# Gate products on quarters of the array and a half-array second score pass in a hybrid RG-LRU and attention step

## The chip, the cores and the metric

The kernel runs on one core of a Trainium2 chip. The metric is device time in microseconds (us) of one execution; the lower the better. Five engines of the core work side by side and wait for one another through semaphores: TensorE (PE in the profile, with its weight loads listed apart as PEld), VectorE (DVE), ScalarE (ACT), GpSimd (POOL) and SyncE (SP), which issues most of the DMAs. TensorE is an array of 128 rows by 128 columns. A product loads a stationary operand into the array (a weight load) and streams a moving operand through it; the contraction runs over the rows, that is over the partitions of both operands, and each column of the array gives one partition of the output, in an accumulation memory called PSUM. PSUM has eight banks of 128 partitions by 512 float32 values here.

## The reference

One inference step of one layer over 2048 prompt tokens and 8 decode tokens, model width 1024. What matters for this change:

```python
z = einsum('btd,de->bte', rmsnorm(x), w_in)
xr, gr, q, k, v = split(z)             # 512, 512, 512, 128, 128 columns
# recurrence group: 8 blocks of 64 channels
xc = causal_conv(xr)
r = sigmoid(block_diag(xc, gate_a_w) + gate_a_b)   # each block its own 64x64 matrix
i = sigmoid(block_diag(xc, gate_x_w) + gate_x_b)
a = exp(-8 * r * softplus(-lru_lambda))
h = scan(h * a + sqrt(1 - a**2) * (i * xc))
rec = h * gelu(gr)
# attention group: 8 heads of 64, 2 key/value heads, window 128, learned sinks
s = einsum(q, k) / 8                   # per head, 128 queries against 256 keys
att = softmax(concat(mask(s), sink)) @ v
h = x + concat(rmsnorm(rec), rmsnorm(att)) @ w_out
y = h + (silu(rmsnorm(h) @ w_gate) * (rmsnorm(h) @ w_up)) @ w_down
```

A final normalisation gives the outputs, beside the new key/value windows and recurrence states.

## The kernel before

Activations are held with channels on partitions and tokens along the free axis. The tokens are worked through in four groups `s` (520 tokens in the first, as two column blocks of 260; 512 in each of the other three). For each group there are 14 units of the input projection (`unit`, matmuls at L281 to L283), a recurrence chain for each of four chunks `c` of 128 channels (`rec_chunk`), attention in items of 128 queries and one key/value head (`attn_item`, 32 items), and the output projection. The feed-forward part follows, from about 620 us on, in three groups of two column halves; the change does not touch it.

Large products are made from rounded pieces: an operand x is split into a rounded part (hi) and the rest (lo), both in a float32 format that TensorE takes in one instruction, and hi·hi, hi·lo and lo·hi are added in PSUM. Products in plain float32 take two instructions each.

*The gates.* The 64x64 matrices of two neighbouring blocks stand on the diagonal of a 128x128 matrix in `gw`, whose other quarters are zero. For each chunk, gate and column block, L608 makes one full-array float32 product `ps = gw.T @ xc` in the single bank of the pool `ps_m` (`m_tile`), and L610 turns it into `ra` or `ia` with a tanh on ScalarE. The same bank serves several other small products.

*The scores.* For an item, `qst` holds four heads' queries with the hi part on the 64 partitions `hr` of its key/value head and the lo part on the other 64 (`lr`). `KK` holds the keys' hi part on both halves of the partitions, so one 128-row product (L767) gives hi·hi + lo·hi. `KL` holds the keys' lo part on `hr` and zeros on the other half, so the second 128-row product (L768) adds hi·lo. The scores of two heads share a bank of the pool `ps_s` (two banks, `s_tile`): heads 0 and 1 in the first, 2 and 3 in the second. L771 on VectorE scales and masks them out of PSUM.

*What sets the order.* All pieces of work are Python generators, each with planned times (`T_IP`, `D_REC`, `D_ATT` and others) that become priorities; `with ahead()` raises a product's priority by a fixed lead. A list scheduler then simulates the program and puts out on each engine the ready instruction of the best priority. What is written in sequence can so be separated in an engine's queue if an operand or a bank of one part is ready later. Each engine works through its queue in the order that comes out.

Of the kernel before, what the change touches and what calls it, by code (L numbers as in the profile page):

```python
# [12 lines left out]
P = 128  # L13
# [177 lines left out]
def hybrid_step(tc, xT, xR, vecs, cst, gatew, win, wout, wgate, wup, wdown, kT, vC, ck, cv, sconv, sh0,  # L191
# [4 lines left out]
    with ExitStack() as ctx:  # L196
# [26 lines left out]
        def o_tile(name):  # L223
            return ps_o.tile([P, 512], F32, tag="o", name=name)

        def m_tile(name):
            return ps_m.tile([P, 512], F32, tag="m", name=name)

# [211 lines left out]
        with ExitStack() as actx:  # L440
# [3 lines left out]
            ap2 = A(tc.tile_pool(name="ap2", bufs=2))  # L444
            ap3 = A(tc.tile_pool(name="ap3", bufs=2))

            gw = ap1.tile([P, 1024], F32, name="gw")
            hist = ap1.tile([P, CR, 3], F32, name="hist")
            nc.vector.memset(hist, 0.0)
            carry = ap1.tile([P, CR], F32, name="carry")  # L450
# [2 lines left out]
            sh = ap1.tile([P, CR, NB], F32, name="sh")  # L453
            KK = ap1.tile([P, 2, 640], F32R, name="KK")
            KL = ap1.tile([P, 2, 640], F32R, name="KL")
            nc.gpsimd.memset(KL[64:128, 0, :].bitcast(F32), 0.0)
            nc.gpsimd.memset(KL[0:64, 1, :].bitcast(F32), 0.0)
            qraw = ap1.tile([P, G, TM], F32, name="qraw")
            rrec = ap1.tile([P, CR, TM], F32, name="rrec")
            ratt = ap1.tile([P, CR, TM], F32, name="ratt")  # L460
# [116 lines left out]
            def rec_chunk(s, c):  # L577
                _, T, nbl, _, _ = SUBS[s]
                prev = (("h", s - 1, c),) if s else ("prologue",)
                yield (ip_time(s, c) - 9,) + ((("xr", s - 1, c),) if s else ())  # L580
                xr = ap3.tile([P, TM + 3], F32, tag="xr", name=f"xr{s}_{c}")
                nc.gpsimd.tensor_copy(xr[:, 0:3], hist[:, c, :])
                yield from unit(s, c, xr[:, 3:])
                t = ip_time(s, c) + U_IP
                yield t
                nc.gpsimd.tensor_copy(hist[:, c, :], xr[:, 512:515])
                fire(("xr", s, c))
                cw = [col(V_CW + c * 4 + j) for j in range(4)]
                xc = rt("xc", f"xc{s}_{c}")
                nc.scalar.activation(xc[:, :512], xr[:, 0:512], AF.Identity, bias=col(V_CB + c), scale=cw[0])  # L590
                if T > 512:
                    nc.scalar.activation(xc[:, 512:T], scv[:, c, 0, :], AF.Identity, bias=col(V_CB + c), scale=cw[0])
                for j in (1, 2, 3):
                    n = T if j == 3 else 512
                    nc.vector.scalar_tensor_tensor(xc[:, :n], xr[:, j:j + n], cw[j], xc[:, :n], ALU.mult, ALU.add)
                    if T > 512 and j < 3:
                        nc.vector.scalar_tensor_tensor(xc[:, 512:T], scv[:, c, j, :], cw[j], xc[:, 512:T],
                                                       ALU.mult, ALU.add)
                if T > 512:
                    nc.scalar.dma_start(sconv_o[:, c, 2, :], xr[:, 515:515 + NB])  # L600
                yield (t + D_REC[0], "prologue")
                ra = rt("ra", f"ra{s}_{c}")
                ia = rt("ia", f"ia{s}_{c}")
                for gi, (dst, hb) in enumerate(((ra, hab), (ia, hxb))):
                    for n0, nn in nbl:
                        ps = m_tile(f"g{s}_{c}_{gi}_{n0}")
                        with ahead():
                            nc.tensor.matmul(ps[:, :nn], gw[:, (gi * 4 + c) * P:(gi * 4 + c + 1) * P], xc[:, n0:n0 + nn],  # L608
                                             start=True, stop=True)
                        nc.scalar.activation(dst[:, n0:n0 + nn], ps[:, :nn], AF.Tanh, bias=hb[:, c:c + 1], scale=0.5)  # L610
                yield t + D_REC[1]
                ix = ap2.tile([P, TM], F32, tag="ix", name=f"ix{s}_{c}")
                nc.vector.scalar_tensor_tensor(ix[:, :T], ia[:, :T], 1.0, xc[:, :T], ALU.add, ALU.mult)
                pair = (s, c >> 1)
                second = pair in q2s
                a = ia if second else ap1.tile([P, TM], F32, tag="a", name=f"a{s}_{c}")
                if not second:
                    q2s[pair] = q2_tile(f"q2{s}_{c >> 1}")
                q2 = q2s[pair][:, c & 1, :]
                nc.scalar.activation(a[:, :T], ra[:, :T], AF.Exp, bias=nc2[:, c:c + 1], scale=nc2[:, c:c + 1])  # L620
                nc.scalar.activation(ra[:, :T], ra[:, :T], AF.Tanh, bias=c2[:, c:c + 1], scale=c2[:, c:c + 1])
                nc.scalar.square(q2[:, :T], a[:, :T])
                nc.vector.scalar_tensor_tensor(q2[:, :T], q2[:, :T], 1.0, ra[:, :T], ALU.add, ALU.mult)
                if second:
                    yield pair_time(s, c) + T_REC
                    both = q2s[pair][:, :, :T]
                    nc.scalar.activation(both, both, AF.Sqrt)
                    fire(("sqrt",) + pair)
                yield (pair_time(s, c) + T_REC + 2 * (c & 1), ("sqrt",) + pair, ("gr", s, c)) + prev
                nc.vector.scalar_tensor_tensor(ix[:, :T], q2[:, :T], 0.5, ix[:, :T], ALU.mult, ALU.mult)  # L630
                h = q2
                nc.vector.tensor_tensor_scan(h[:, :512], a[:, :512], ix[:, :512],
                                             carry[:, c:c + 1], ALU.mult, ALU.add)
                nc.gpsimd.tensor_copy(carry[:, c:c + 1], h[:, 511:512])
                if T > 512:
                    nc.vector.tensor_tensor(h[:, 512:T], a[:, 512:T], sh[:, c, :], ALU.mult)
                    nc.vector.tensor_tensor(h[:, 512:T], h[:, 512:T], ix[:, 512:T], ALU.add)
                    nc.scalar.dma_start(sh_o[:, c, :], h[:, 512:T])
                gr = rrec[:, c, :]
                nc.vector.scalar_tensor_tensor(gr[:, :T], gr[:, :T], 0.5, h[:, :T], ALU.mult, ALU.mult)  # L640
                fire(("h", s, c))
# [51 lines left out]
            def k_chunk(s):  # L693
# [10 lines left out]
                nc.vector.tensor_copy(KK[0:64, 1, m], kr[64:128, :512])  # L704
                nc.vector.tensor_tensor(KL[0:64, 0, m], kr[0:64, :512], KK[0:64, 0, m].bitcast(F32), ALU.subtract)
                nc.vector.tensor_tensor(KL[64:128, 1, m], kr[64:128, :512], KK[64:128, 1, m].bitcast(F32), ALU.subtract)
                if s == 3:
                    nc.scalar.dma_start(pkT, kr[:, 384:512])
                if s == 0:
# [30 lines left out]
            def attn_item(s, b, kv, t):  # L740
# [9 lines left out]
                qst = ap3.tile([P, G, P], F32R, tag="qst", name=f"qst{gb}_{kv}")  # L750
                nc.scalar.copy(qst[hr], qraw[hr, :, qs])
                nc.vector.tensor_tensor(qst[lr], qraw[hr, :, qs], qst[hr].bitcast(F32), ALU.subtract)
                if last:
                    fire(("qdone", s))
                yield (t + D_ATT[0], "prologue")
# [1 line left out]
                mx = ap2.tile([P, 2, G], F32, tag="mx", name=f"mx{gb}_{kv}")  # L757
                ns = nsk[:, kv * G:kv * G + G]
                nc.gpsimd.tensor_copy(sc[:, :, kn:kn + 1], ns.unsqueeze(2))
                for g2 in range(2):  # L760
                    ps = s_tile(f"s{gb}_{kv}_{g2}")
                    for gi in range(2):
                        g = g2 * 2 + gi
                        o = ps[:, gi * 256:gi * 256 + kn]
                        ks = slice(b * P + k0, b * P + k0 + kn)
                        with ahead():
                            nc.tensor.matmul(o, qst[:, g, :], KK[:, kv, ks], start=True, stop=False)  # L767
                            nc.tensor.matmul(o, qst[:, g, :], KL[:, kv, ks], start=False, stop=True)  # L768
                    for gi in range(2):
                        g = g2 * 2 + gi  # L770
                        nc.vector.tensor_tensor_reduce(  # L771
                            sc[:, g, :kn], ps[:, gi * 256:gi * 256 + kn], mask[:, k0:k0 + kn], -SCALE, ns[:, g:g + 1],
                            ALU.add, ALU.min, accum_out=mx[:, 0, g:g + 1])
                if last:
                    fire(("sdone", s))
                yield t + D_ATT[1]
# [580 lines left out]


_INS = [
    ("xT", (P, KD, NTOK)), ("xR", (NTOK, D)), ("vecs", (P, NV)), ("cst", (P, 384)), ("gatew", (P, 1024)),  # L1360
    ("win", (14, P, 1024)), ("wout", (8, P, 1024)), ("wgate", (NF, P, 1024)), ("wup", (NF, P, 1024)),
    ("wdown", (NF, P, 1024)), ("kT", (P, NB * P)), ("vC", (P, NB * P)), ("ck", (NB, 127, P)),
    ("cv", (NB, 127, P)), ("sconv", (P, CR, 3, NB)), ("sh0", (P, CR, NB)),
# [17 lines left out]
def layout_inputs(inputs):  # L1381
# [5 lines left out]
    def units(w):  # L1387
# [23 lines left out]
    k = np.arange(P)[None]  # L1411
    cst = np.concatenate([np.eye(P, dtype=f32), np.where(k >= q, 0.0, NEG), np.where(k <= q, 0.0, NEG)],
                         axis=1).astype(f32)
    gatew = np.zeros((P, 8, P), f32)
    for gi, n in enumerate(("gate_a_w", "gate_x_w")):
        for c in range(CR):
            for j in range(2):
                r = slice(j * HD, j * HD + HD)
                gatew[r, gi * 4 + c, r] = i[n][0, 2 * c + j]
    ckw, cvw = i["cache_k_win"][0].reshape(NB, P, P), i["cache_v_win"][0].reshape(NB, P, P)  # L1420
    arr = dict(
        xT=x.T.reshape(KD, P, NTOK).transpose(1, 0, 2), xR=x, vecs=vecs, cst=cst, gatew=gatew.reshape(P, 1024),
        win=units(win), wout=units(wout), wgate=units(i["w_gate"][0]), wup=units(i["w_up"][0]),
        wdown=i["w_down"][0].reshape(NF, P, D),
        kT=ckw.transpose(2, 0, 1).reshape(P, NB * P), vC=cvw.transpose(1, 0, 2).reshape(P, NB * P),
# [32 lines left out]
```

## Time and profile before

| | us |
|---|---|
| median of 2 runs | 2077.37 |
| lowest and highest run | 2076.76, 2077.98 |
| span of the profiled execution | 2070.1 |
| end of the recurrence and attention part, about | 620 |
| feed-forward part, about | 1450 |

The span runs from the first to the last instruction of one profiled execution; the run times also hold what lies around it, so the two differ by 7.3 us.

In the page, a line such as "PE 2017.5 (97%) x12238" gives an engine's busy time, its share of the span and its number of instructions. A line of the timeline gives the start, the duration, the engine, the source line, the operation, the output and input tiles, the part of the array (rows by columns), the shape of the moving operand and the number of merged instructions; in square brackets stands the idle time in front of it and what ended it. The durations of matmuls hold the pipeline, so consecutive matmuls overlap in it, and the distance between starts tells what one costs. A line that groups instructions gives the count, the summed and the mean duration, then the idle time in front of them and what ended most of it.

### The profile page before, as it was taken

To read this page: it belongs to the slowest core of one execution; us is meant where nothing else is said; L and a number is where in the kernel's file an instruction comes from. 1 tells how busy PE (TensorE), PEld (TensorE's weight loads), DVE (VectorE), ACT (ScalarE), POOL (GpSimd) and SP (SyncE) were. 2 spreads that over 40 slices of the span, in tenths; PEclk is the share of its full clock that TensorE was granted. 3 is DMA by queue.
4 is the path that set the end of the run, shared out by engine and by line. 5 is a ranking of instruction groups with operands and counts; after the bars stand their busy time and mean duration, and the time that the engine had idled before them with its cause. 6 is when DMAs were issued, how large, how long until landed. Compare 5 with 4: busy or idle time off the path is not lost.

```text
span 2070.1 us, 35112 instructions
## 1 busy us (share of the span) xinstructions
PE 2017.5 (97%) x12238; PEld 1904.3 (92%) x12238; DVE 1565.5 (76%) x2947; ACT 894.2 (43%) x1822; POOL 935.3 (45%) x820
## 2 busy tenths in 40 slices
PE   8999899999999999999999999999999999999997
PEld 8988787878777899999999999999999999999997
DVE  6786886766985967776756688788778778888786
ACT  5774684563663543333334432233235433333332
POOL 5211342030123788667766844455446523422332
PEclk9999999999999999999999999999999999999998
DMA  8764484576678856565646687676667676556652
GB/s 308 262 205 159 158 295 166 190 242 208 203 255 279 315 197 218 206 221 195 213 174 211 225 278 240 218 242 211 229 225 250 243 239 196 183 190 198 198 179 90
DMA packets 208993, 450.99 MB, mean 218 GB/s; under 512 B 25232, under 2 KB 82720, under 8 KB 208800
## 3 DMA queue, kind: packets, MB, share of 16 engines
q1 hardware_dynamic: 205616, 446.24, 64.3%
q10 hardware_dynamic: 3200, 2.51, 0.4%
q8 instruction: 97, 1.59, 0.3%
q14 instruction: 80, 0.66, 0.1%
HBM read 335.89 MB, written 113.84 MB: 217 GB/s over the span
## 4 chain that ended last, share of the span: by engine, by line
PE 66%; DVE 8%; DMA 6%; issue 2%; ACT 1%; POOL 1%; SPq 0%; DVEq 0%; POOLq 0%; ACTq 0%
PE ps_u L1222 6%; PE ps_u L1224 6%; PE ps_u L1223 6%; PE ps_g L1223 5%; PE ps_g L1224 5%; PE ps_g L1222 5%; PE pd L1261 3%; PE pd L1263 3%; PE pd L1262 3%; PE pw L1288 3%; PE pw L1289 3%; PE pw L1290 3%; DMA n<-hs 2%; PE ip L281 2%; PE ip L282 2%
## 5 line engine op out<-in xcount | busy, mean ns | idle before, releaser
L1222 PE MATMUL ps_g<-hn,w_g 128*128 128x342 f32 (+1 forms) x924 | 295.4, 320 | 1.9 <-DVE xres L942 1.8
L1223 PE MATMUL ps_g<-hn,w_g 128*128 128x342 f32 (+1 forms) x924 | 296.0, 320 | 0.5 <-DVE hn L433 0.5
L1222 PE MATMUL ps_u<-hn,w_u 128*128 128x342 f32 (+1 forms) x924 | 295.0, 320 | 0.9 <-DVE y L1294 0.6
L1224 PE MATMUL ps_g<-hn,w_g 128*128 128x342 f32 (+1 forms) x924 | 295.7, 320 | 0.0
L1223 PE MATMUL ps_u<-hn,w_u 128*128 128x342 f32 (+1 forms) x924 | 295.0, 319 | 0.0
L1224 PE MATMUL ps_u<-hn,w_u 128*128 128x342 f32 (+1 forms) x924 | 293.7, 319 | 0.0
L1294 DVE TENSOR_TENSOR y<-y,pw 128x342 f32<-128x342 f32 x504 | 237.6, 503 | 49.5 <-PE pw L1290 47.9
L281 PE MATMUL ip<-xn,w_in 128*128 128x512 f32 (+1 forms) x560 | 199.8, 362 | 8.6 <-ACT xn L286 8.6
L282 PE MATMUL ip<-xn,w_in 128*128 128x512 f32 (+1 forms) x560 | 201.2, 361 | 0.4 <-DVE xn L287 0.4
L283 PE MATMUL ip<-xn,w_in 128*128 128x512 f32 (+1 forms) x560 | 199.4, 357 | 0.0
L1222 PEld LDWEIGHTS ps_g<-hn,w_g 128*128 128x128 f32 x924 | 174.3, 189 | 2.7 <-DVE xres L942 2.0
L1222 PEld LDWEIGHTS ps_u<-hn,w_u 128*128 128x128 f32 x924 | 174.1, 189 | 1.7 <-DVE y L1294 1.1
L1223 PEld LDWEIGHTS ps_g<-hn,w_g 128*128 128x128 f32 x924 | 174.5, 189 | 1.2 <-DVE hn L433 0.9
L1224 PEld LDWEIGHTS ps_g<-hn,w_g 128*128 128x128 f32 x924 | 174.6, 189 | 0.2 <-DVE w_g L1030 0.2
L1223 PEld LDWEIGHTS ps_u<-hn,w_u 128*128 128x128 f32 x924 | 174.2, 189 | 0.0
L1224 PEld LDWEIGHTS ps_u<-hn,w_u 128*128 128x128 f32 x924 | 174.0, 189 | 0.0
L1212 DVE TENSOR_TENSOR c_u<-c_u,ps_u 128x342 f32<-128x342 f32 (+1 forms) x231 | 113.6, 506 | 76.5 <-PE ps_u L1224 74.6
L1195 POOL TENSOR_TENSOR c_u<-c_u,c_g 128x342 f32<-128x342 f32 (+1 forms) x60 | 59.1, 984 | 217.6 <-DVE c_u L1212 204.2
L1265 DVE TENSOR_TENSOR y<-y,pd 128x344 f32<-128x344 f32 (+1 forms) x240 | 115.8, 507 | 50.1 <-PE pd L1263 47.8
L1263 PE MATMUL pd<-fh,w_d 128*128 128x344 f32 (+1 forms) x480 | 153.5, 320 | 0.1
L1261 PE MATMUL pd<-fh,w_d 128*128 128x344 f32 (+1 forms) x480 | 152.8, 321 | 0.6 <-DVE y L1265 0.4
L1262 PE MATMUL pd<-fl,w_d 128*128 128x344 f32 (+1 forms) x480 | 153.2, 319 | 0.0
(302 smaller groups left out, 5384.8 us busy)
## 6 DMA issues: line engine op xcount, KB each, us to landing
w_g<-split_g SPq DMA_DIRECT2D x88, 512.0 KB, 4.2
w_u<-split_u SPq DMA_DIRECT2D x88, 512.0 KB, 4.8
w_in<-split_w SPq DMA_DIRECT2D x84, 512.0 KB, 3.4
rg<-in_wgate SPq DMA_DIRECT2D x110, 256.0 KB, 3.1
ru<-in_wup SPq DMA_DIRECT2D x110, 256.0 KB, 3.4
w_out<-split_w SPq DMA_DIRECT2D x48, 512.0 KB, 4.5
split_g<-w_g SPq DMA_DIRECT2D x44, 512.0 KB, 2.9
split_u<-w_u SPq DMA_DIRECT2D x44, 512.0 KB, 3.5
```

The costliest lines, as they stand in the source:

```text
L281: nc.tensor.matmul(out, wh, xh, start=first, stop=False)
L282: nc.tensor.matmul(out, wh, xl, start=False, stop=False)
L283: nc.tensor.matmul(out, wl, xh, start=False, stop=last)
L1212: nc.vector.tensor_tensor(o, a, b, op)
L1222: nc.tensor.matmul(ps, wh, hi, start=kk == 0, stop=False)
L1223: nc.tensor.matmul(ps, wh, lo, start=False, stop=False)
L1224: nc.tensor.matmul(ps, wl, hi, start=False, stop=kk == 3)
L1261: nc.tensor.matmul(ps, w[:, 0, c:c + P], hi, start=h == 0, stop=False)
L1262: nc.tensor.matmul(ps, w[:, 0, c:c + P], lo, start=False, stop=False)
L1263: nc.tensor.matmul(ps, w[:, 1, c:c + P], hi, start=False, stop=h == 1)
L1265: nc.vector.tensor_tensor(ys[gi, n, m], ys[gi, n, m], ps, ALU.add)
L1294: nc.vector.tensor_tensor(v, v, ps, ALU.add)
```

## The change

The gate weights lose their zero quarters: `gatew` holds the 64x64 matrices side by side, on rows 0 to 63 for the first block and 64 to 127 for the second. For each chunk and column block there are now four products of 64 rows by 64 columns, one on each quarter of the array: gate a from rows 0 to 63 into output partitions 0 to 63 and from 64 to 127 into 64 to 127 (bank `pa`, from `ps_m`), gate x from rows 0 to 63 into partitions 64 to 127 and the other way round (bank `px`, from `ps_acc`, the pool with three banks that the projections use). ScalarE takes `ra` out of `pa` in one activation, and `ia` out of `px` in two, which swap the halves back.

In the scores, the 128-row first products stay. For the second pass, `KL` has the keys' lo part on both halves of its partitions (two more ScalarE copies per token group, no zero-fills), and a new tile `qh2` has the hi part of heads 2 and 3 on the partitions `lr` (one ScalarE copy per item). Each of the four second products contracts over 64 rows: heads 0 and 1 on the rows `hr`, heads 2 and 3 on the rows `lr`, written so that one product of either kind follows the other, into different banks.

```diff
+        def gate_tile(name):
+            return acc_tile(name)
...
-            gw = ap1.tile([P, 1024], F32, name="gw")
+            gw = ap1.tile([P, 512], F32, name="gw")
...
-            nc.gpsimd.memset(KL[64:128, 0, :].bitcast(F32), 0.0)
-            nc.gpsimd.memset(KL[0:64, 1, :].bitcast(F32), 0.0)
...
-                for gi, (dst, hb) in enumerate(((ra, hab), (ia, hxb))):
-                    for n0, nn in nbl:
-                        ps = m_tile(f"g{s}_{c}_{gi}_{n0}")
-                        with ahead():
-                            nc.tensor.matmul(ps[:, :nn], gw[:, (gi * 4 + c) * P:(gi * 4 + c + 1) * P], xc[:, n0:n0 + nn],
+                for n0, nn in nbl:
+                    pa, px = m_tile(f"ga{s}_{c}_{n0}"), gate_tile(f"gx{s}_{c}_{n0}")
+                    with ahead():
+                        for r0, ps, c0 in ((0, pa, 0), (64, pa, 64), (0, px, 64), (64, px, 0)):
+                            w0 = (4 * (ps is px) + c) * 64
+                            nc.tensor.matmul(ps[c0:c0 + 64, :nn], gw[r0:r0 + 64, w0:w0 + 64], xc[r0:r0 + 64, n0:n0 + nn],
                                              start=True, stop=True)
-                        nc.scalar.activation(dst[:, n0:n0 + nn], ps[:, :nn], AF.Tanh, bias=hb[:, c:c + 1], scale=0.5)
+                    nc.scalar.activation(ra[:, n0:n0 + nn], pa[:, :nn], AF.Tanh, bias=hab[:, c:c + 1], scale=0.5)
+                    for r0, c0 in ((0, 64), (64, 0)):
+                        nc.scalar.activation(ia[r0:r0 + 64, n0:n0 + nn], px[c0:c0 + 64, :nn], AF.Tanh,
+                                             bias=hxb[r0:r0 + 64, c:c + 1], scale=0.5)
...
+                nc.scalar.copy(KL[64:128, 0, m], KL[0:64, 0, m].bitcast(F32))
+                nc.scalar.copy(KL[0:64, 1, m], KL[64:128, 1, m].bitcast(F32))
...
+                qh2 = ap3.tile([P, 2, P], F32R, tag="qh2", name=f"qh2{gb}_{kv}")
+                nc.scalar.copy(qh2[lr], qraw[hr, 2:4, qs])
...
-                for g2 in range(2):
-                    ps = s_tile(f"s{gb}_{kv}_{g2}")
+                pss = [s_tile(f"s{gb}_{kv}_{g2}") for g2 in range(2)]
+                ks = slice(b * P + k0, b * P + k0 + kn)
+                with ahead():
                     for gi in range(2):
-                        g = g2 * 2 + gi
-                        o = ps[:, gi * 256:gi * 256 + kn]
-                        ks = slice(b * P + k0, b * P + k0 + kn)
-                        with ahead():
-                            nc.tensor.matmul(o, qst[:, g, :], KK[:, kv, ks], start=True, stop=False)
-                            nc.tensor.matmul(o, qst[:, g, :], KL[:, kv, ks], start=False, stop=True)
+                        for g2 in range(2):
+                            nc.tensor.matmul(pss[g2][:, gi * 256:gi * 256 + kn], qst[:, g2 * 2 + gi, :], KK[:, kv, ks],
+                                             start=True, stop=False)
+                        for g2, q, rows in ((0, qst[hr, gi, :], hr), (1, qh2[lr, gi, :], lr)):
+                            nc.tensor.matmul(pss[g2][:, gi * 256:gi * 256 + kn], q, KL[rows, kv, ks],
+                                             start=False, stop=True)
```

The rest of the diff loops over the four heads for L771, as before, and lays out the smaller `gatew` on the host.

More of the change, by code (lines that the diff above doesn't have):

```diff
@@ L759, in attn_item @@
                 nc.gpsimd.tensor_copy(sc[:, :, kn:kn + 1], ns.unsqueeze(2))
-                for g2 in range(2):
-                    ps = s_tile(f"s{gb}_{kv}_{g2}")
+                pss = [s_tile(f"s{gb}_{kv}_{g2}") for g2 in range(2)]
+                ks = slice(b * P + k0, b * P + k0 + kn)
+                with ahead():
                     for gi in range(2):
-                        g = g2 * 2 + gi
-                        o = ps[:, gi * 256:gi * 256 + kn]
-                        ks = slice(b * P + k0, b * P + k0 + kn)
-                        with ahead():
[L767 to L773, printed above, removed]
+                        for g2 in range(2):
[4 more added lines that the diff above has]
+                                             start=False, stop=True)
+                for g in range(G):
+                    nc.vector.tensor_tensor_reduce(
+                        sc[:, g, :kn], pss[g // 2][:, g % 2 * 256:g % 2 * 256 + kn], mask[:, k0:k0 + kn], -SCALE,
+                        ns[:, g:g + 1], ALU.add, ALU.min, accum_out=mx[:, 0, g:g + 1])
                 if last:
@@ L1359 @@
 _INS = [
-    ("xT", (P, KD, NTOK)), ("xR", (NTOK, D)), ("vecs", (P, NV)), ("cst", (P, 384)), ("gatew", (P, 1024)),
+    ("xT", (P, KD, NTOK)), ("xR", (NTOK, D)), ("vecs", (P, NV)), ("cst", (P, 384)), ("gatew", (P, 512)),
     ("win", (14, P, 1024)), ("wout", (8, P, 1024)), ("wgate", (NF, P, 1024)), ("wup", (NF, P, 1024)),
@@ L1413, in layout_inputs @@
                          axis=1).astype(f32)
-    gatew = np.zeros((P, 8, P), f32)
+    gatew = np.zeros((P, 8, HD), f32)
     for gi, n in enumerate(("gate_a_w", "gate_x_w")):
@@ L1418, in layout_inputs @@
                 r = slice(j * HD, j * HD + HD)
-                gatew[r, gi * 4 + c, r] = i[n][0, 2 * c + j]
+                gatew[r, gi * 4 + c] = i[n][0, 2 * c + j]
     ckw, cvw = i["cache_k_win"][0].reshape(NB, P, P), i["cache_v_win"][0].reshape(NB, P, P)
     arr = dict(
-        xT=x.T.reshape(KD, P, NTOK).transpose(1, 0, 2), xR=x, vecs=vecs, cst=cst, gatew=gatew.reshape(P, 1024),
+        xT=x.T.reshape(KD, P, NTOK).transpose(1, 0, 2), xR=x, vecs=vecs, cst=cst, gatew=gatew.reshape(P, 512),
         win=units(win), wout=units(wout), wgate=units(i["w_gate"][0]), wup=units(i["w_up"][0]),
```

## The prediction

> **What bounds the kernel now.** I read the page's busy times first, then busy time by stretch, then the products by shape, then the tensor engine's timeline where the changed products stand.
>
> ```profile
> span 2070.1 us, 35112 instructions
> PE 2017.5 (97%) x12238; PEld 1904.3 (92%) x12238; DVE 1565.5 (76%) x2947; ACT 894.2 (43%) x1822; POOL 935.3 (45%) x820
> ```
>
> Stretches (length, then busy us of PE, PEld, DVE, ACT, POOL, then the granted clock):
>
> ```profile
> 0.00:10.00 10.00, 1.73 (x6) 1.44 (x7) 1.98 (x8) 5.85 (x10) 5.48 (x11) 1.00 0.80 267
> 250.00:300.00 50.00, 45.60 (x330) 41.73 (x331) 45.00 (x86) 43.63 (x89) 26.24 (x24) 0.97 0.88 302
> 0.00:620.00 620.00, 593.62 (x3328) 502.56 (x3329) 469.87 (x1024) 368.44 (x786) 162.88 (x182) 0.99 0.66 221
> ```
>
> TensorE bounds it: 97% of the span. All that the change touches lies in the first 620 us (projections, recurrence, attention). There TensorE idles 620 − 593.6 = 26.4 us, 8.3 of them in the first 10 us before any product can start, so 18.1 us later on. ScalarE works 368 of the 620 us. So what a product takes on TensorE goes almost wholly into the span, and the sum below is one of TensorE time. The span is 2070.1 us and the median of the runs 2077.4; I add 7.3 us at the end.
>
> **What the products cost today.** The durations of the matmul rows overlap, so I take start to start. Gate products (L608), at 260 and at 512 columns; each is one row of two instructions, and the start printed for the row behind is too early, so I go to the row after that and subtract that row's own spacing (0.12 and 0.23 us):
>
> ```profile
> 40.00 0.28 PE L281 MATMUL ip<-xn,w_in 128*128 128x260 f32 x1
> 40.12 0.60 PE L608 MATMUL g<-xc,gw 128*128 128x260 f32 x2
> 40.37 0.47 PE L282 MATMUL ip<-xn,w_in 128*128 128x260 f32 x1
> 40.68 0.28 PE L283 MATMUL ip<-xn,w_in 128*128 128x260 f32 x1
> ...
> 352.11 1.02 PE L608 MATMUL g<-xc,gw 128*128 128x512 f32 x2
> 352.56 0.80 PE L282 MATMUL ip<-xn,w_in 128*128 128x512 f32 x1
> 353.20 0.40 PE L283 MATMUL ip<-xn,w_in 128*128 128x512 f32 x1
> 353.43 0.39 PE L281 MATMUL ip<-xn,w_in 128*128 128x512 f32 x1
> ```
>
> That is 40.68 − 0.12 − 40.12 = 0.44 us and 353.20 − 0.23 − 352.11 = 0.86 us, so u = 0.22 and 0.43 us per instruction. Second score products (L768):
>
> ```profile
> 107.06 0.28 PE L767 MATMUL s<-KK,qst 128*128 128x256 f32 x1
> 107.17 0.28 PE L768 MATMUL s<-KL,qst 128*128 128x256 f32 x1
> 107.29 0.28 PE L767 MATMUL s<-KK,qst 128*128 128x256 f32 x1
> 107.41 0.28 PE L768 MATMUL s<-KL,qst 128*128 128x256 f32 x1
> ```
>
> 0.115 us each. The whole prize is small: 16 gate products of 260 columns and 24 of 512 are 7.0 + 20.6 = 27.7 us, 128 second score products 14.7 us; halving both would give 21 us, 1%.
>
> **Step 1: in which order the smaller products run.** A saving needs products on different parts of the array next to each other in TensorE's queue. The instruction order of the changed program has this for a typical attention item:
>
> ```
> L774 s_1_0<-KK,qst    L777 s_1_0<-KL,qst
> L774 s_1_0<-KK,qst    L777 s_1_0<-KL,qst
> (five input-projection products, some others)
> L774 s_1_1<-KK,qst    L777 s_1_1<-KL,qh
> L774 s_1_1<-KK,qst    L777 s_1_1<-KL,qh
> ```
>
> The diff writes the two halves behind one another, but they go to two PSUM banks which come free at different times, and the scheduler issues the first bank's four products before the second's. Counted over the program: 92 of the 128 64-row score products stand alone between 128-row products, 36 form 18 pairs. The 80 gate quarters form 24 groups (11 of four, 10 of two, 2 of six, one of four on only two quarters); 14 groups have 512 columns, 10 have 260. So TensorE goes from the 128-row form to a smaller one and back 92 + 18 + 24 = 134 times.
>
> **Step 2: what such a change of form costs.** Before has just two products on 64 rows, in the decode part (L854, L855). TensorE's rows, then the weight loads', then the producers of L854's operands:
>
> ```profile
> 169.72 0.39 PE L281 MATMUL ip<-xn,w_in 128*128 128x512 f32 x1
> 170.04 0.27 PE L854 MATMUL dS<-cs,dw 64*128 64x64 f32 x1
> 170.24 0.50 PE L282 MATMUL ip<-xn,w_in 128*128 128x512 f32 x1
> 170.67 0.43 PE L855 MATMUL dS<-dw,ones 64*128 64x64 f32 x2
> 171.03 0.50 PE L283 MATMUL ip<-xn,w_in 128*128 128x512 f32 x1
> 171.36 0.39 PE L281 MATMUL ip<-xn,w_in 128*128 128x512 f32 x1
> ```
>
> ```profile
> 169.48 0.19 PEld L281 LDWEIGHTS ip<-xn,w_in 128*128 128x128 f32 x1
> 170.03 0.13 PEld L854 LDWEIGHTS dS<-cs,dw 64*128 64x128 f32 x1 [0.36 <-issue]
> 170.24 0.19 PEld L282 LDWEIGHTS ip<-xn,w_in 128*128 128x128 f32 x1
> ```
>
> ```profile
> 168.21 0.28 DVE L850 TENSOR_SCALAR dw<-dw,dm 64x129 f32<-64x129 f32 x1
> ```
>
> L281's load began at 169.48, a whole product ahead of its use. L854's should have begun at 169.72 in the same way; its operand was ready at 168.49, yet it began at 170.03, 0.08 us after L281's 0.23 us had run out (169.95). L282's load came only behind L854 again. L282's row is 0.11 us longer than usual (0.50 against 0.39), so its real start is 170.24 + 0.10 = 170.34: one small product of 64 columns took 170.34 − 169.95 = 0.39 us. L855 with two instructions: L282 ran to 170.57, L283 started at 171.36 − 0.23 = 171.13, so 0.56 us, 0.17 more for the second instruction. I read it as: no weights are loaded ahead across a change of rows. The Trainium skill says so against this change: in "TensorEngine Tiling (Array Packing)", Key Properties, changing the tiling mode, not just the tile, drains the TensorE. These rows agree, with 0.39 us for a product that alone would be hidden.
>
> **Step 3: the sum.** A lone 64-row score product: 0.39 plus 0.09 for 192 more columns (0.12 us per 260) = 0.48 in place of 0.115, so +0.36 us; × 92 = +33.1. A pair: 0.48 − 0.23 = +0.25 if the second runs beside the first; if behind it, 0.17 + 0.09 more, +0.51. I take the middle, 0.38 × 18 = +6.8 (4.5 to 9.2).
>
> A gate group pays the change too: 0.39 less 0.03 for its 64 columns, and 0.06 less for a weight load of half as many columns (from 0.11, the smallest spacing above), 0.30 × 24 = +7.2. Inside a group: a quarter product is still two instructions on one quarter, the second of which must follow the first, and rows start in program order. So only the second of one overlaps the first of the next: m quarters take (m + 1)u where the full products took m·u. That is one u per group: 14 × 0.43 + 10 × 0.22 = +8.2. Bounds: all quarters at once make a group of four 2u (−9.9 in all), no overlap 2m·u (+27.7).
>
> ScalarE gets 20 more gate activations, since half the partitions take as long as all, 32 copies of 64x256 (qh2) and 8 of 64x512 (KL):
>
> ```profile
> L610 ACT ACTIVATE ia<-g,hxb 128x512 f32<-128x512 f32 x12 | 8.2, 681 | 7.2 <-PE g L608 7.1
> L610 ACT ACTIVATE ia<-g,hxb 128x260 f32<-128x260 f32 x8 | 3.8, 472 | 2.9 <-PE g L608 2.9
> L778 ACT ACTIVATE sc<-sc,mx 128x129 f32<-128x129 f32 x8 | 3.2, 396 | 0.0
> L778 ACT ACTIVATE sc<-sc,mx 128x257 f32<-128x257 f32 x116 | 57.9, 502 | 15.1 <-DVE mx L771 14.2 <-POOL sc L759 0.6
> L751 ACT CAST qst<-qraw 64x512 fp32r<-64x512 f32 x32 | 19.7, 616 | 20.1 <-DVE qraw L572 13.7 <-PE s L768 6.0
> ```
>
> About 12 × 0.68 + 8 × 0.47 + 32 × 0.45 + 8 × 0.62 = 31 us, in a part where ScalarE idles 252. The new wait (TensorE for qh2) stands behind the first products of the item and hides there; uncovered, 32 × 0.45 = 14 us. The gate's second product leaves the single m bank for one of the three banks of the projections; its quick release rests on ScalarE, and a unit of 24 products takes 24 × 0.23 = 5.5 us, which covers one activation. Against that, waits of the old order go:
>
> ```profile
> PE g L608 <- ACT ra L610: 4.2, 3, 2.2
> ```
>
> These 4.2 us were the second gate waiting for the one bank. With TensorE later by 8% in this part, other waits shorten too, and ScalarE's work makes new ones; of the 18.1 us idle I count 5 as absorbed (0 to 12). The smaller weight transfer and the two zero-fills at the start cost and give nothing: TensorE waits there for its first inputs. DVE's work does not change in length.
>
> Forecast: 33.1 + 6.8 + 7.2 + 8.2 − 5 = +50 us; 2070.1 + 50 + 7.3 = 2127 us. From 2113 to 2140 with the bounds of pairs and absorption and a tenth of doubt on the one price of 0.36 us.
>
> **The rivals.** *Quarters all at once:* a group of four takes one product's 2u. The Trainium skill has this in "TensorE: Matmul & The Clock Gate", Part 3: a pack lasts one matmul plus some 4 ns per further tile. No row here shows two tiles running together. Sum: 33.1 + 4.5 + 7.2 − 9.9 − 5 = +30, 2107 us. Against it stands the two-instruction form. *No overlap at all:* 33.1 + 9.2 + 7.2 + 27.7 − 5 = +72, 2150 us; nothing excludes it. *The other side, no price for the form:* the 0.36 us of L854 belongs to the decode part (its weight load follows a bare wait), and in the stream loads are pulled ahead as usual. Then −9.9 for the gates and −0.115 × 18 for the pairs give 2065 us; with the in-order gates (+8.2) about 2083. It decides below 12/134 = 0.09 us per change; measured are 0.36 and, at L855, as much again, so it is unlikely. *ScalarE becomes late in attention:* in 250 to 300 us it is already busy 43.6 of 50. Where qh2's copy is not hidden, up to 14 us more: 2140.
>
> **How the numbers follow.** Forecast 0.54, quarters at once 0.18, no overlap 0.12, no price 0.10, late ScalarE 0.06. 2% of the time before is 41.5 us, up to 2118.9, about what a measurement of this kernel can tell from no change. Four fifths of the forecast's chance lie above (0.43), with 0.12 and 0.06 that is 0.61 slower. Within 2%: 0.11 + 0.18 + 0.09 = 0.38. Faster by over 2% would need 2036, more than the whole prize: 0.01. The range leaves out the case without a price and the top of the case without overlap: 2098 to 2152.
>
> **What would show it.** In the changed profile: weight loads of the 64-row score products starting some 0.08 us behind the product before, and the next load behind them; 0.45 to 0.5 us of TensorE per lone score product; gate groups of 512 columns lasting 5u + 0.3 = 2.4 us (1.2 if at once, 3.7 if not overlapped); the part after 620 us as long as before, only later. Wrong if the loads of 64-row products run ahead as the others do, or if TensorE's idle time grows by more than a few us.

## The result and the profile after

The changed kernel takes 2139.12 us (2138.56 to 2139.68) against 2077.37 us, a ratio of 1.031 (95% interval 1.029 to 1.033): 61.8 us slower. The forecast was 2127 us, slower by 50, in a range of 2098 to 2152.

The page of the changed kernel, span and busy times:

```profile
span 2136.8 us, 35376 instructions
PE 2070.7 (97%) x12318; PEld 1919.5 (90%) x12318; DVE 1557.4 (73%) x2947; ACT 927.8 (43%) x1882; POOL 931.0 (44%) x818
```

The spans of the two profiled executions lie 66.7 us apart, the medians 61.8; the readings below are of the profiled executions. The time around a span is about 2 us in every run that has both figures (2138.56 against 2136.8 here), so most of the 7.3 us between span and median of the kernel before is something else: its profiled execution was some 5 us shorter than its timed ones. A difference between a profiled execution and that of the kernel before is therefore about 5 us too large, or more. The feed-forward part begins at 685.4 us in the kernel before, not at about 620, and at 753.9 us in the changed one; "the first part" below is what lies ahead of it. Busy time by stretch up to there and from there on, first of the kernel before, then of the changed one (length, then PE, PEld, DVE, ACT, POOL, the granted clock, DMA):

```profile
0.00:685.40 685.40, 658.17 (x3626) 554.44 (x3627) 512.14 (x1097) 394.83 (x839) 188.18 (x200) 0.99 0.68 225
685.40:2070.10 1384.70, 1359.28 (x8613) 1349.88 (x8611) 1053.35 (x1851) 499.35 (x983) 747.13 (x621) 0.99 0.64 214
```

```profile
0.00:753.90 753.90, 710.01 (x3695) 566.36 (x3696) 503.73 (x1100) 429.82 (x902) 186.03 (x198) 0.95 0.61 205
753.90:2136.80 1382.90, 1360.64 (x8625) 1353.13 (x8623) 1053.67 (x1848) 497.96 (x980) 745.00 (x621) 0.99 0.63 214
```

All of the loss is in the first part (+68.5 us); the feed-forward part is no longer than before (1382.9 against 1384.7). In the first part TensorE is busy 51.8 us longer, idles 43.9 us in place of 27.2, and its mean granted clock falls from 0.99 to 0.95.

**The scores.** An item's products in the changed kernel, on TensorE and then as weight loads:

```profile
96.25 0.28 PE L284 MATMUL ip<-xn,w_in 128*128 128x260 f32 x1
96.37 0.28 PE L774 MATMUL s<-KK,qst 128*128 128x256 f32 x1
96.58 0.38 PE L777 MATMUL s<-KL,qst 64*128 64x256 f32 x1
96.89 0.38 PE L774 MATMUL s<-KK,qst 128*128 128x256 f32 x1
97.21 0.38 PE L777 MATMUL s<-KL,qst 64*128 64x256 f32 x1
97.52 0.39 PE L285 MATMUL ip<-xn,w_in 128*128 128x260 f32 x1
97.74 0.28 PE L286 MATMUL ip<-xn,w_in 128*128 128x260 f32 x1
```

```profile
96.25 0.19 PEld L774 LDWEIGHTS s<-KK,qst 128*128 128x128 f32 x1
96.58 0.18 PEld L777 LDWEIGHTS s<-KL,qst 64*128 64x128 f32 x1
96.89 0.19 PEld L774 LDWEIGHTS s<-KK,qst 128*128 128x128 f32 x1
97.20 0.18 PEld L777 LDWEIGHTS s<-KL,qst 64*128 64x128 f32 x1
97.52 0.19 PEld L285 LDWEIGHTS ip<-xn,w_in 128*128 128x128 f32 x1
97.62 0.19 PEld L286 LDWEIGHTS ip<-xn,w_in 128*128 128x128 f32 x1
```

The first load (96.25) still begins a product ahead, together with the projection's product. Every load behind it changes the form (the part of the array that is used, 128 rows or 64) and begins only when the product before has streamed: 96.37 + 0.115 = 96.49, load at 96.58. So each of the four now takes 0.31 us, and the group, from 96.37 to the real start of the projection behind it (97.74 − 0.12 = 97.62), 1.25 us in place of 4 × 0.115. Two lone 64-row products, that is ones without a second 64-row product beside them, cost 0.79 us more, 0.39 each.

**The gates.** A group of four quarters with 512 columns in the changed kernel:

```profile
383.32 0.40 PE L286 MATMUL ip<-xn,w_in 128*128 128x512 f32 x1
383.64 0.65 PE L610 MATMUL ga<-xc,gw 64*64 64x512 f32 x2
383.65 0.65 PE L610 MATMUL gx<-xc,gw 64*64 64x512 f32 x2
384.12 0.59 PE L610 MATMUL ga<-xc,gw 64*64 64x512 f32 x2
384.13 0.60 PE L610 MATMUL gx<-xc,gw 64*64 64x512 f32 x2
384.66 0.50 PE L284 MATMUL ip<-xn,w_in 128*128 128x512 f32 x1
385.00 0.39 PE L285 MATMUL ip<-xn,w_in 128*128 128x512 f32 x1
```

Each quarter product is two instructions. The first instructions of all four quarters start within 0.02 us, the second ones 0.48 us later, again together. From 383.55 (383.32 + 0.23) to 384.77 (385.00 − 0.23) it is 1.22 us, where two full products took 2 × 0.86.

### The profile page after: what moved, and what is told of

Read it like the earlier page. It is cut to its first block, busy times and chain, and to the rows that moved or that the text cites. A ratio compares the mean times of both kernels' runs of the same rounds, so it can differ in the third digit from the quotient of the medians.

```text
span 2136.8 us, 35376 instructions
## 1 busy us (share of the span) xinstructions
PE 2070.7 (97%) x12318; PEld 1919.5 (90%) x12318; DVE 1557.4 (73%) x2947; ACT 927.8 (43%) x1882; POOL 931.0 (44%) x818
## 4 chain that ended last, share of the span: by engine, by line
PE 79%; DVE 10%; DMA 5%; issue 2%; ACT 2%; POOL 1%; SPq 0%; DVEq 0%; ACTq 0%; POOLq 0%
PE ps_u L1231 6%; PE ps_u L1232 6%; PE ps_u L1233 6%; PE ps_g L1232 6%; PE ps_g L1233 6%; PE ps_g L1231 6%; PE ip L284 4%; PE ip L285 4%; PE ip L286 3%; PE pd L1270 3%; PE pd L1272 3%; PE pd L1271 3%; PE pw L1297 3%; PE pw L1299 3%; PE pw L1298 3%
## 5 line engine op out<-in xcount | busy, mean ns | idle before, releaser
L284 PE MATMUL ip<-xn,w_in 128*128 128x512 f32 (+1 forms) x560 | 200.0, 362 | 11.5 <-ACT xn L289 8.3
L1107 POOL TENSOR_TENSOR wd<-rd,wd 128x512 fp32r<-128x512 f32 x72 | 100.6, 1398 | 108.3 <-ACT wd L1106 100.0
```

What stands on the lines that cost most here:

```text
L284: nc.tensor.matmul(out, wh, xh, start=first, stop=False)
L1107: eng((E_DLO1, E_DLO2)[gi - 1][j]).tensor_tensor(w[:, :, 1], v, w[:, :, 0].bitcast(F32), op=ALU.subtract)
```

## The experiments

Ratios are to the kernel before on the same chip, with 95% intervals. An edit can also change the order that the scheduler gives the whole first part. Of the edits to the kernel before, x1_rows alone leaves TensorE's order as it was. In y1_bank, y2_halves, y3_diag, y4_full and z3_late it is another one from an early instruction on (between the 189th and the 328th of some 3600), so their costs hold that of the new order too.

**x1_rows.** The kernel before with the zero rows left out of the second score product, nothing else:

```diff
-nc.tensor.matmul(o, qst[:, g, :], KL[:, kv, ks], start=False, stop=True)
+nc.tensor.matmul(o, qst[hr, g, :], KL[hr, kv, ks], start=False, stop=True)
```

> The kernel before, with only this edit: the second score product contracts over the 64 rows that hold the keys' lo part and leaves out the 64 rows of zeros (same result). No new copies on ScalarE, gates untouched, 128 lone 64-row products. Theory A (each change between 128-row and 64-row products stops the loading of weights ahead, some 0.4 us per lone product as seen in the changed kernel's trace): 128 x 0.395 = +50 us, 2115 to 2145 us with some clock loss, and the weight loads behind the product before, not beside it. Rival B (the loss came from the new order, the new ScalarE copies and the new waits): at most +10 us, 2070 to 2088.

Measured: 2108.48 us, 1.014 (1.012 to 1.016), +29.7 us. That is between the two: the price of the form is there without any other edit, and with TensorE's 3626 instructions of the first part in the same order as before, but not all of it reaches the end. Its first part by stretch:

```profile
0.00:719.30 719.30, 700.88 (x3626) 569.92 (x3627) 510.75 (x1097) 398.18 (x840) 187.95 (x200) 0.99 0.65 215
```

TensorE is busy 42.7 us more than before (700.9 against 658.2), less than 128 × 0.39 = 50: over the whole first part a lone product costs 0.33 us on average, while 0.39 is the price in an unbroken stream of full-array products. TensorE idles 18.4 us in place of 27.2, so nearly 9 us of waits go. The clock stays at 0.99.

**x2_gates.** The kernel before with the gate part of the change (its diff is in the section on the change) and the scores as before.

> The kernel before with the gate part of the change alone; scores as before. Theory A (four quarters run at once, a group of 512 columns takes 1.22 us where two products took 1.72): the gates save 6 us and little else changes, 2065 to 2077 us. Rival C (the gate part brings the new idle time of TensorE and the half clock, through its place in the queue and the bank it takes from the projections): 2090 to 2115 us, with idle time in front of gate or projection products.

Measured: 2124.06 us, 1.021 (1.019 to 1.023), +45.3 us, above the ranges of both. Theory A falls: the gate part alone costs more than the score part alone. In the first part TensorE idles 58.0 us (733.2 − 675.2) in place of 27.2. What TensorE waited for, of that run (total us, times, longest):

```profile
PE o L807 <- DVE ratt L812: 10.9, 6, 2.9
...
PE ga L612 <- DVE xc L598: 6.8, 4, 3.8
PE o L807 <- ACT pth L799: 5.8, 2, 4.3
PE o L808 <- DVE ptl L800: 4.0, 3, 1.9
PE ga L612 <- issue: 3.5, 1, 3.5
PE pt L796 <- DVE ptl L800: 2.9, 3, 1.7
PE ip L284 <- DVE qraw L575: 2.9, 1, 2.9
```

Rows of all three kinds are there: gates in front of their input (ga behind xc), the projection in front of a bank that is not free (ip behind the emptying of qraw), and attention products behind VectorE and ScalarE.

**x4_gate_o.** x2_gates with gate x in the attention's output bank (`return o_tile(name)` in `gate_tile`).

> The gate part of the change alone, with gate x in the bank of the attention outputs in place of one of the projections' three banks. If the bank taken from the projections makes TensorE wait (rival C, in its form by banks), this is at least 5 us faster than the gate part alone; if the bank doesn't matter, within 3 us of it; if waiting for the attention's bank holds the gate products up, slower.

Measured: 2136.84 us, 1.028 (1.025 to 1.030). Slower than x2_gates by 13 us: sparing the projections' bank at the attention's expense is worse.

**y1_bank, y2_halves, y3_diag, y4_full** take the gate part to pieces. y1: full products, one activation, second bank. y2: one bank, halved activation. y3: one bank, one activation, two diagonal quarters per product. y4: all of the gate part except the quarters.

```diff
 # y1_bank
+pa, px = m_tile(f"ga{s}_{c}_{n0}"), acc_tile(f"gx{s}_{c}_{n0}")
+for gi, ps in ((0, pa), (1, px)):
+    nc.tensor.matmul(ps[:, :nn], gw[:, (gi * 4 + c) * P:(gi * 4 + c + 1) * P], xc[:, n0:n0 + nn], ...)
 # y2_halves, for gate x
+for r in (slice(0, 64), slice(64, 128)):
+    nc.scalar.activation(ia[r, n0:n0 + nn], ps[r, :nn], AF.Tanh, bias=hxb[r, c:c + 1], scale=0.5)
 # y3_diag
+for r0 in (0, 64):
+    w0 = (gi * 4 + c) * P + r0
+    nc.tensor.matmul(ps[r0:r0 + 64, :nn], gw[r0:r0 + 64, w0:w0 + 64], xc[r0:r0 + 64, n0:n0 + nn], ...)
```

> The kernel before with full-array gate products and one activation each, but with gate x in one of the projections' three banks and both gates issued per column block, as in the change. Theory D (the loss of the gate part is the second bank: it lets the gate products stand earlier in TensorE's queue, in front of their inputs, and takes a bank from the projections): 2110 to 2130 us, with the gates' wait for xc and the idle time of the gate part. Rival E (the halved activations on ScalarE) and rival F (the quarters themselves): 2070 to 2085 us.

> The kernel before with one edit: the activation of gate x is made in two halves of 64 partitions, 20 instructions and some 12 us more on ScalarE; same products, same banks. Theory D: 2075 to 2085 us. Rival E: 2100 to 2125 us.

> The kernel before with each full gate product replaced by the two 64x64 products on its diagonal quarters, same bank, same single activation. The two run at once, so the products take as long as before; what is added is the change of form, about 40 times 0.3 to 0.4 us, 12 to 16 us less what the idle time takes up. Theory D: 2080 to 2095 us. Rival F (quarters cost much by themselves, 40 us and more): 2110 us or over.

> The gate part of the change (second bank, swapped halves, halved activations) with full-array products in place of the quarters; the difference to the gate part alone is the quarters themselves. Theory D: 2120 to 2140 us, a few us slower than the gate part alone, whose groups of four quarters are shorter. Rival F: 2070 to 2090 us. Rival E: as the halved activations alone.

| run | us | ratio and interval | above the kernel before, us |
|---|---|---|---|
| y1_bank | 2112.55 | 1.016 (1.014 to 1.018) | 32.7 |
| y2_halves | 2097.12 | 1.009 (1.007 to 1.011) | 17.3 |
| y3_diag | 2096.39 | 1.008 (1.007 to 1.010) | 16.5 |
| y4_full | 2118.80 | 1.019 (1.017 to 1.020) | 38.9 |

Theory D holds for the greater part: the second bank with full products, and the order that comes with it, makes 33 of the gate part's 45 us. The halved activations in the kernel before cost 17 us, more than theory D allowed, though TensorE's waits for the gates' bank did not grow (2.6 us where they were 4.2); how much of the 17 comes from the new order isn't known. On top of the second bank they cost only 6 (y4 less y1). y3 lies 1 us above theory D's range: 16.5 us over 40 changes is 0.41 each, where undisturbed groups in its trace show 0.35, about 14 us in all. Whether the quarters gain or lose in place of full products isn't decided: x2_gates lies 6 us further above its kernel before than y4_full, and the intervals of the two ratios overlap. TensorE's waits in y1_bank:

```profile
PE ga L608 <- DVE xc L595: 7.5, 5, 2.2
PE o L801 <- DVE ratt L806: 6.1, 6, 2.0
PE o L801 <- ACT pth L793: 4.6, 4, 2.1
PE s L768 <- DVE mx L772: 4.4, 2, 3.8
PE bc_at L319 <- POOL atcols L309: 4.2, 1, 4.2
PE ga L608 <- issue: 4.0, 1, 4.0
PE ip L281 <- DVE qraw L572: 3.9, 1, 3.9
PE pt L790 <- DVE ptl L794: 2.7, 1, 2.7
PE ip L281 <- ACT ia L611: 2.6, 1, 2.6
```

The gates wait 11.5 us for xc (the row with "issue" is the first group: VectorE writes xc until 37.03, the product starts at 37.14), projections 6.5 us for a bank (the row that names ia is the bank gate x has just left), the rest is attention. The first gate product is TensorE's 189th instruction in the trace; in the kernel before it is the 247th, at 40.12 us, and waits for nothing. (The expectations have 178 and 236 by another count; the distance is the same.) That the single bank had kept the gate products behind their inputs is read from this order; no run shows it apart from the bank itself. The first part of y1_bank:

```profile
0.00:724.10 724.10, 673.51 (x3626) 565.26 (x3627) 503.69 (x1097) 399.17 (x839) 190.32 (x200) 0.96 0.64 213
```

It is 38.7 us longer than in the kernel before: 23.4 us are idle time (50.6 against 27.2), and 15.3 us are longer busy time of the same products on the full array, at a granted clock of 0.96 in place of 0.99.

**z3_late.** y1_bank with `t + D_REC[0] + 8` as the gates' planned time and `ahead(0)` in place of `ahead()`.

> The run with the second bank alone (full products, one activation each; it took 2112.6 us), with the gates planned 8 us later and without the lead over other products, so that they stand further back in TensorE's queue (the first near place 242 in place of 178, 236 in the kernel before). Theory D1 (the loss of the second bank is the gates' place in front of their inputs): the gates' wait for xc and the half clock behind it go, 2080 to 2100 us. Theory D2 (the bank missing from the projections): within 5 us of 2112. If the gates come too late for the recurrence, slower.

Measured: 2117.02 us, 1.018 (1.015 to 1.020). Nothing gained. The first gate product is now TensorE's 253rd instruction and no longer waits, but later ones still wait 7.8 us for xc, and attention products wait more. The time lies in the range of theory D2, within 5 us of 2112, and outside D1's. But the waits that D1 said would go did not go, so a blanket delay doesn't mend the order, and this doesn't separate the gates' place from the missing bank.

**x5_pairs.** The changed kernel with each score product held in program order (`keep`), bank 1 before bank 0, so that the two halves stand together.

> The changed kernel with the score products of an item held in program order, the bank that comes free last written first, so that the two 64-row products stand next to each other: 61 pairs and 8 single ones in place of 18 pairs and 92 single ones. Theory A (the price is per change of form): 69 changes at about 0.4 us less what a pair saves, about 20 us less than the changed kernel, 2110 to 2125 us; the second product of a pair starts within some 20 ns of the first if the halves of the array work at once. Rival B (order and ScalarE): 2130 to 2150 us.

Measured: 2223.73 us, 1.070 (1.067 to 1.072), far outside both. The held order made TensorE idle 97.8 us in its first part (824.1 us long, 726.3 busy), and the granted clock there was 0.91. So no run shows a gain from pairs. But this one shows what they cost; TensorE's rows:

```profile
466.04 0.40 PE L286 MATMUL op<-mix,w_out 128*128 128x512 f32 x1
466.28 0.39 PE L774 MATMUL s<-KK,qst 128*128 128x256 f32 x2
466.60 0.38 PE L777 MATMUL s<-KL,qh 64*128 64x256 f32 x1
466.60 0.38 PE L777 MATMUL s<-KL,qst 64*128 64x256 f32 x1
466.91 0.51 PE L774 MATMUL s<-KK,qst 128*128 128x256 f32 x2
467.35 0.38 PE L777 MATMUL s<-KL,qh 64*128 64x256 f32 x1
467.35 0.38 PE L777 MATMUL s<-KL,qst 64*128 64x256 f32 x1
467.67 0.50 PE L284 MATMUL op<-mix,w_out 128*128 128x512 f32 x1
468.00 0.39 PE L285 MATMUL op<-mix,w_out 128*128 128x512 f32 x1
```

The two halves start together and the second is free. From 466.28 to 467.77 the eight products take 1.49 us against 8 × 0.118 = 0.94: a pair costs 0.27 us more than two full products, because it still changes the form twice.

**a1_scores.** The score part whole, with y3_diag's gates.

> The score part of the change whole (64-row products on both halves, the copies on ScalarE), with the gates as two diagonal 64x64 products in one bank with one activation each, which alone took 2096.4 us (16.5 over the kernel before). If the score part costs what its 64-row products cost, as in the run that only drops the rows of zeros (30 us), 2120 to 2130 us. If the ScalarE copies and the two banks taken at once add to it, over 2135; if the pairs repay a part, under 2118.

Measured: 2126.42 us, 1.022 (1.020 to 1.024), +45.4; less y3's 16.5 that is 29, the same as x1_rows' 30. The ScalarE copies for qh2 and KL and the two banks taken together add nothing that shows; a few us could hide, since the interval is some 4 us to either side and a1_scores has 16 pairs where x1_rows has lone products only. No run here beat the kernel before.

## Why the prediction was right, and where only by offset

*The order.* Right: the trace has the 92 lone 64-row products and 18 pairs that were read from the instruction order.

*The price of the form.* Right. Forecast +0.36 us for a lone product and 0.38 for a pair, measured 0.39 and 0.27 in undisturbed rows; 92 × 0.39 + 18 × 0.27 = 40.7 us where 39.9 were forecast, or 35 with the 0.33 that x1_rows gives on average. x1_rows shows it alone, and that it comes with the change of form, not with ScalarE or the order. It also shows that waits take up some 9 us of it.

*The gates' products.* The step that failed is "only the second of one overlaps the first of the next": the quarters' first instructions run all together, then their second ones. This was the rival *quarters all at once*. Read on undisturbed groups, multiplied by their number, and set against what the full products took: 10 groups of four at 512 columns −0.50 us each, 4 pairs at 512 and 6 at 260 +0.34 each, the other four groups together about +0.1; in all −1.5 us, where the forecast had +15.4 (7.2 + 8.2) and the rival −2.7. The Trainium skill says in "TensorE: Matmul & The Clock Gate", Part 3, that a pack lasts one matmul plus some 4 ns per further tile. The trace agrees for each round of four: its starts lie within 0.02 us, and the second round follows 0.48 us after the first, where one instruction on the full array takes 0.43.

*The absorbed waits.* Also wrong, and the other way. Forecast was that 5 us of idle time go; idle time grew by 16.7 us. The prediction had named idle time that grows by more than a few us as a sign that it is wrong, and here it was. The reason given, that "These 4.2 us were the second gate waiting for the one bank", saw the wait but not that with a second bank the gate products stand in front of their inputs. y1_bank shows that the second bank, with full products, costs 33 us. How it divides between the gates' earlier place, the bank taken from the projections and the new order of all the rest stays open.

*The clock* wasn't in the forecast as a term. In the changed kernel, the wait in front of the first gate group, and the stretches from 30 to 50 us:

```profile
34.20 0.28 PE L286 MATMUL ip<-xn,w_in 128*128 128x260 f32 x1
37.97 0.70 PE L610 MATMUL ga<-xc,gw 64*64 64x260 f32 x2 [3.48 <-issue]
```

```profile
30.00:40.00 10.00, 6.52 (x51) 5.17 (x49) 5.49 (x14) 3.51 (x7) 3.91 (x6) 0.84 0.90 315
40.00:50.00 10.00, 10.00 (x67) 9.44 (x68) 5.18 (x11) 7.52 (x16) 3.00 (x3) 0.82 0.29 98
```

Behind 3.5 us of idling the granted clock is 0.84 and 0.82 over the next stretches, while TensorE is busy from 40 to 50 without a break. Of the 68.5 us that the first part got longer, 40.7 − 1.5 are the products by form and 16.7 idle time; the remaining 12.6 fit the lower clock. With 0.33 us for a lone product 18 us would remain. That the clock can cost that much y1_bank shows: its full-array products, the same as in the kernel before, kept TensorE busy 15.3 us longer. In the clock records of the traces, each of which is 1.0 or 0.5, the first part has 17.1 us at 0.5 in the kernel before and in x1_rows, 58.0 in y1_bank and 75.1 in the changed kernel.

*ScalarE.* The rival priced qh2's copies; these cost nothing that shows (a1_scores). The halved gate activations, which the forecast counted as ScalarE time without a cost, came with 17 us in y2_halves and 6 on top of the second bank.

So the direction and the largest term, 40 of the 50 us, were right. That the total came near is partly luck: a gate term 17 us too high stood in for idle time, 22 us off, and a clock term of 13 to 18 us that was missing.

## What to carry to other kernels

A product on 64 rows of the array pays for leaving the full form and for coming back; here that was 0.39 us for one that cost 0.115, so such products can pay only where the built order puts them together (groups of four quarter products of 512 columns gained 0.50 us, groups of two lost 0.34), and that order has to be read, not the source. Where a scheduler sets the order, a single shared buffer may be what holds work back until its inputs are there: before freeing it, ask where the freed work will stand in its engine's queue. Price the pieces of a change one at a time on the chip: here the two parts cost 30 and 45 us alone and 62 together. With both, TensorE idled 43.9 us in the first part, with the gates alone 58.0; and 36 of the 128 second products stood in pairs, where x1_rows has lone ones only. And compare the orders with and without an edit before putting a cost down to the edit alone.

## What the runs showed of the hardware

Two products on different halves of the array's rows, into different banks, start at the same time to 0.01 us (466.60 in x5_pairs), and four on its quarters within 0.02 us (383.64 in the changed kernel), also where two of them write different partitions of one bank. A change between 128 and 64 rows costs some 0.2 us each way: the weights are no longer loaded ahead (load at 96.58, 0.09 us behind the end of the product before). A 64-row product slows the full-array product behind it as much as itself (0.31 us each where both took 0.115). Not every change of rows does this: in the kernel before, the load of a product on 104 rows (bc_x) begins at 32.26, a whole product ahead of its use at 32.38. In the changed kernel the granted clock was at 0.5 from 36.86 to 43.69 us: it fell within the idle time of 3.5 us that ended at 37.97, and stayed there for 5.7 us of busy time.
